# Where a product's weights lie, and in which order high and low parts are multiplied: two edits to a transformer block on one core

## The chip, the core and the metric

The kernel runs on one core of a Trainium2 chip. The metric is device time in microseconds (us) of one execution. The kernel before takes 967.7 us, the median of three runs from 967.39 to 967.99.

A core has a matrix engine (TensorE, PE in the profile; its loading of weights is listed apart as PEld), a vector engine (VectorE, DVE), a scalar engine (ScalarE, ACT), a general engine (GpSimd, POOL) and a queue engine (SyncE, SP) that issues loads. They work side by side and wait for each other through semaphores. Matrix products accumulate in banks of a memory called PSUM; the other tiles lie in SBUF, 128 partitions wide.

## The reference

One layer over 256 tokens of width 2048, all in float32:

```python
h = rmsnorm(x, norm1_g)
q, k, v, u = split(h @ w_in)               # 1536, 512, 512, 512 columns
a = rmsnorm(window_attention(q, k, v, sink))
f = rmsnorm(fourier_mix(u, w_fourier))
x = x + concatenate([a, f]) @ w_out
h = rmsnorm(x, norm2_g)
gate, val = split(h @ w_up)                # 5504 columns each
gate = conv3(gate) + dw_b                  # along the tokens
x = x + (gelu(gate) * val) @ w_down
y = rmsnorm(x, normf_g)
```

Most of the arithmetic is in the four large products: w_in, w_out, w_up and w_down.

## The kernel before

**Float32 products out of parts.** TensorE multiplies a rounded 32-bit format here. So each float32 weight tile is split into a high part (ScalarE copies it into the rounded format, L170 or L910) and a low part (VectorE subtracts the high part from the raw tile, L171 or L911), and so is each activation. A product is the sum of three: high by high, low by high, high by low.

**Where the parts lie.** A weight tile is 128 x 2048. Its two parts share one tile of 2 x 2048 + 128 elements a partition, of which there are three in turn (parts_tile, L138). How many elements the high part is moved in from the tile's start, and the low part from the middle, is a table of four kinds of use:

```python
PLACES = {"still": (0, 16), "first": (16, 16), "moving": (0, 0), "product": (28, 28)}
```

**Two ways to multiply.** In moving_weights (L303) the activation is the stationary operand and 512 columns of weights stream past it, three matmuls for each 128 rows of weights (L309 high by high, L310 low by high, L311 high by low). In still_weights (L315) the weights are stationary and the activation streams: for each of 16 k tiles of 128 rows one matmul of 512 columns with the weights' high part (L320; the 512 are the activation's 256 high and 256 low columns) and one of 256 columns with their low part (L321; the high columns alone). The two halves of the 512 are added when the bank is emptied. All go into one PSUM bank, the first clearing it.

**The stages, in order.** u and v with moving weights; then 16 units of still weights for k and q, one k and three q for each of four groups, with the attention's small products (scores, transposes, values) and the Fourier mix's placed between the units; then w_out with moving weights in 16 steps; then the feed-forward part.

**The feed-forward part** is a written list of items (ff_items, L64). 86 of them are up-projections (gate and val of 43 tiles, still weights, L1105). 56 are products of the down-projection (L1109): w_down for the first 32 tiles is taken in four groups, and each group by a scheme of seven products per column half (names P1, P7, N5, N3, P6, P2, N4) whose operands are sums of blocks. by_parts (L1010) multiplies one: its four blocks take three matmuls of 512 columns each (L1014 to L1016), with the operand stationary. Items 0 and 1 are gate0 and val0, item 2 is gate1, which stands behind four small float32 matmuls that spread the second norm's scales (L293). The list goes on with still units up to val7, and then each group opens with three of them and alternates product and still unit ("uuu" + "su" * 13 + "s"). Behind the four groups come four late down-projections with moving weights, six more still units, four more late down-projections and the last columns.

**What sets the order around it.** Each engine runs its instructions in the order written. Behind each item on TensorE ff_step (L941) empties earlier banks, splits the weights of the item two further on and issues the loads for later ones on SP's queue; some products' sums of raw weights are made by accumulating loads on POOL's queue (L915, L917, L926). At the end of a column half shared_out (L996) adds eight 128 x 512 tiles on VectorE.

The functions that the edit touches:

Of the kernel before, what the change touches and what calls it, by code (L numbers as in the profile page):

```python
# [15 lines left out]
S = 256  # L16
NK = D // P
# [46 lines left out]
def ff_items():  # L64


    def ups(tiles):
        return [(kind, j) for j in tiles for kind in ("gate", "val")]

    items = ups(range(8))  # L70
    for g in range(N_GROUPS):
        todo = {
            "u": ups(range(8 * g + 8, 8 * g + 16)),
            "s": [("product", g, c, p) for c in range(2) for p in PRODUCTS[c]],
        }
        items += [todo[c].pop(0) for c in PATTERN]
        assert not any(todo.values())
    items += [("down", 0, c) for c in range(4)] + ups(LAST)
    items += [("down", 1, c) for c in range(4)] + [("last", c) for c in range(4)]
    return items  # L80
# [3 lines left out]
def block_kernel(  # L84
# [18 lines left out]
    nc = tc.nc  # L103
# [10 lines left out]
    def bank(pool, name):  # L114
        return pool.tile([P, 512], F32, tag=pool.name, name=name)
# [5 lines left out]
    items, up_index = ff_items(), {}  # L121
# [11 lines left out]
    raws, halves = {}, {}  # L133


    PLACES = {"still": (0, 16), "first": (16, 16), "moving": (0, 0), "product": (28, 28)}

    def parts_tile(name, place):  # L138
        t = wp.tile([P, 2 * 2048 + 128], F32R, tag="parts", name=name, bufs=3)
        oh, ol = PLACES[place]  # L140
        return t[:, oh : oh + 2048], t[:, 2048 + ol : 4096 + ol]

    def load(i, pieces=1):
        if i < len(units) and i not in raws:
            src, n, _ = units[i]
            raws[i] = wp.tile([P, 2048], F32, tag="raw", name=f"raw{i}", bufs=RAW)
            m = n // pieces
            for p in range(pieces):
                s = slice(p * m, (p + 1) * m)
                nc.sync.dma_start(raws[i][:, s], src[:, s])  # L150
                yield
# [50 lines left out]
    first = load(0, 4)  # L202
# [50 lines left out]
    ps = bank(dn, "ps_warm")  # L253
# [49 lines left out]
    def moving_weights(hi, lo, n, kk, act, b, ps, first, last, q0=0):  # L303

        for q, k in enumerate(kk, q0):
            ah = act(k)[:, b * P : (b + 1) * P]
            al = act(k)[:, S + b * P : S + (b + 1) * P]
            wh, wl = hi[:, q * n : (q + 1) * n], lo[:, q * n : (q + 1) * n]
            nc.tensor.matmul(ps, ah, wh, start=first and q == q0, stop=False)  # L309
            nc.tensor.matmul(ps, al, wh, start=False, stop=False)  # L310
            nc.tensor.matmul(  # L311
                ps, ah, wl, start=False, stop=last and q == q0 + len(kk) - 1
            )

    def still_weights(hi, lo, ps, kk):  # L315

        for k in kk:
            h = hT[k // 4][:, k % 4, :]
            s = slice(k * P, (k + 1) * P)
            nc.tensor.matmul(ps, hi[:, s], h, start=k == 0, stop=False)  # L320
            nc.tensor.matmul(  # L321
                ps[:, 0:S], lo[:, s], h[:, 0:S], start=False, stop=k == NK - 1
            )

    def hk(k):
        return hT[k // 4][:, k % 4, :]

    later = []  # L330

# [13 lines left out]
    def at(when, i, f, *a):  # L345
        when.setdefault(i, []).append((f, a))
# [5 lines left out]
    def unit(i, work):  # L352
        run(before, i)
        work(*halves.pop(i))
        run(beside, i)
        step(i)
        run(behind, i)
# [6 lines left out]
    for k in range(NK):  # L364
        c, q = k // 4, k % 4
# [4 lines left out]
        hi, lo = halves[c]  # L370
# [187 lines left out]
    for c in range(4):  # L558

        def work(hi, lo):  # L560
            for b in range(2):
                moving_weights(
                    hi, lo, 512, range(4 * c, 4 * c + 4), hk, b, ps_v[b], c == 0, c == 3
                )

        unit(N_V + c, work)
# [139 lines left out]
    for n, (kind, h) in enumerate(QK_ORDER):  # L706

        def work(hi, lo):
            ps = st["ps", kind, h] = bank(mm, f"ps_{kind}{h}")
            still_weights(hi, lo, ps, range(NK))  # L710

        unit(N_QK + n, work)

# [49 lines left out]
    for n, (c, kq) in enumerate(OUT_ORDER):  # L763
# [15 lines left out]
        if kq >= 2:  # L779
            part = "a" if kq == 2 else "f"  # L780
            ps = ps_a[c] if kq < 3 else ps_a[c, "f"]
# [113 lines left out]
    def ring_load():  # L895
        if ring_next[0] < len(ring):
            key = ring[ring_next[0]]
            ring_next[0] += 1
            ring_tiles[key] = fp.tile([P, 2048], F32, tag="rawd", name="rawd%d%d%s" % key)
            nc.sync.dma_start(ring_tiles[key], weights_of(*key))  # L900
# [20 lines left out]
    def first_sums(g, c):  # L921

        a, b = ring_tiles[g, c, "a"], ring_tiles[g, c, "b"]
        x = ring_tiles["x"] = fp.tile([P, 2048], F32, tag="sumw", name=f"sumw{g}{c}", bufs=1)
        nc.vector.tensor_tensor(x, a, b, ALU.add)
        nc.gpsimd.dma_start(b, weights_of(g, c, "d"), accum_op=ALU.add)  # L926
# [14 lines left out]
    def ff_step(n):  # L941
        todo, later[:] = list(later), []
        for f in todo:
            next(f, None)
        run(beside, n)
        split_item(n + 2)
        for f in todo:
            for _ in f:
                pass
        run(behind, n)  # L950

    def up_posts(n, kind, j, ps):
        if kind == "gate":
            at(beside, n + 1, scaled_sum, ps, f"g{j}")
            at(beside, n + 2, gate_conv, j)
            at(behind, n + 2, gate_gelu, j)
        else:
            at(beside, n + 1, scaled_sum, ps, f"v{j}")
            at(beside, n + 2, val_mult, j)
            if j % 8 == 7 and j < 8 * N_GROUPS:  # L960
                g = j // 8
                at(behind, n + 1, operand, g, "P1")
                at(behind, n + 2, operand, g, "N4")
                at(behind, n + 3, operand_sums, g, 0)
                at(behind, n + 4, operand, g, "P7")
                at(behind, n + 4, operand, g, "P2")
                at(behind, n + 5, operand_sums, g, 1)
                at(behind, n + 5, operand, g, "N5")
                at(behind, n + 6, operand, g, "N3")
                at(behind, n + 7, operand, g, "P6")  # L970
            if j >= 8 * N_GROUPS:
                at(behind, n + 2, act_parts, j)
# [37 lines left out]
    def by_parts(ps, o, hi, lo, first, last):  # L1010

        for p in range(4):
            s = slice(p * 512, (p + 1) * 512)
            nc.tensor.matmul(ps, o[:, 0, p, :], hi[:, s], start=first and p == 0, stop=False)  # L1014
            nc.tensor.matmul(ps, o[:, 1, p, :], hi[:, s], start=False, stop=False)  # L1015
            nc.tensor.matmul(ps, o[:, 0, p, :], lo[:, s], start=False, stop=last and p == 3)  # L1016
# [58 lines left out]
    for q in range(2):  # L1075
        kind, j = items[q]
        ps = bank(mm, f"ps_{kind}{j}")
# [6 lines left out]
    for ps, hi, lo in pair:  # L1084
        still_weights(hi, lo, ps, range(12, NK))
# [7 lines left out]
    for n, it in enumerate(items):  # L1093
        if n < 2:
            continue
        if it[0] == "last":
            break
        if n in (8, 9):
            ring_load()
        if n == 13:  # L1100
            pending.append(lambda: first_sums(0, 0))
        if it[0] in ("gate", "val"):
            kind, j = it
            ps = bank(mm, f"ps_{kind}{j}")
            still_weights(*halves.pop(up_index[n]), ps, range(NK))  # L1105
            ff_step(n)
            up_posts(n, kind, j, ps)
            continue
        if it[0] == "product":  # L1109
            kind, g, c, p = it  # L1110
            end = g == N_GROUPS - 1
            if (c, p) in held:
                by_parts(held[c, p], parts[p], *halves.pop(it), g == 0, end)
            else:
                ps = bank(mm, f"ps_{p}{g}{c}")
                by_parts(ps, parts[p], *halves.pop(it), True, True)
                at(beside, n + 1, product_out, g, c, p, ps)
            if end and p == "N4":
                at(behind, n + 1, shared_out, c)
        else:  # L1120
            kind, g, c = it
            hi, lo = halves.pop(up_index[n])
            ps = [bank(mm, f"ps_l{g}{c}{b}") for b in range(2)]
            for b in range(2):
                moving_weights(hi, lo, 512, LATE[g], act.get, b, ps[b], True, True)
            at(beside, n + 1, down_out, c, ps)
            if (g, c) == (0, 0):
                gfb = fp.tile([P, D], F32, tag="sumw", name="gfb", bufs=1)
                nc.gpsimd.dma_start(gfb, normf_g.partition_broadcast(P))
        ff_step(n)  # L1130
# [149 lines left out]
```

## Time and profile before

| What | Value |
|---|---|
| median of three runs | 967.7 us |
| the profiled execution's own time | 967.03 us |
| its span, first to last instruction | 965.3 us |
| TensorE busy | 955.1 us, 5089 matmuls |
| VectorE busy | 745.0 us |
| ScalarE busy | 540.0 us |
| GpSimd busy | 44.6 us |
| mean granted TensorE clock | 0.998 |
| moved by DMAs | 211.59 MB, mean 219 GB/s |

The page counts an engine as busy while an instruction of it is listed as running. Matmuls overlap, so a busy TensorE may still be issuing more slowly than it could; the distance between the starts of two matmuls is read from the timeline, and a stretch of the table of stretches gives it for many at once. The chain is the work that ended last, followed backwards from releaser to releaser.

### The profile page before, as it was taken

To read this page: it belongs to the slowest core of one execution; us is meant where nothing else is said; L and a number is where in the kernel's file an instruction comes from. 1 tells how busy PE (TensorE), PEld (TensorE's weight loads), DVE (VectorE), ACT (ScalarE), POOL (GpSimd) and SP (SyncE) were. 2 spreads that over 40 slices of the span, in tenths; PEclk is the share of its full clock that TensorE was granted. 3 is DMA by queue.
4 is the path that set the end of the run, shared out by engine and by line. 5 is a ranking of instruction groups with operands and counts; after the bars stand their busy time and mean duration, and the time that the engine had idled before them with its cause. 6 is when DMAs were issued, how large, how long until landed. Compare 5 with 4: busy or idle time off the path is not lost.

```text
span 965.3 us, 12801 instructions
## 1 busy us (share of the span) xinstructions
PE 955.1 (99%) x5089; PEld 820.1 (85%) x5089; DVE 745.0 (77%) x924; ACT 540.0 (56%) x654; POOL 44.6 (5%) x59
## 2 busy tenths in 40 slices
PE   9999999999999999999999999999999999999996
PEld 7789998888888888888888888888888888888885
DVE  5668877666576689787898877988778979878674
ACT  6756766554455446556565555665555655553534
POOL 0000000000000000000000000000000000000003
PEclk9999999999999999999999999999999999999999
DMA  8854444446456676977778787876977686775532
GB/s 320 338 189 155 175 138 168 142 167 215 177 177 243 233 220 194 288 226 256 225 253 240 235 293 231 261 236 206 290 245 245 206 278 213 227 225 210 209 132 88
DMA packets 33548, 211.59 MB, mean 219 GB/s; under 512 B 3792, under 2 KB 4304, under 8 KB 9424
## 3 DMA queue, kind: packets, MB, share of 16 engines
q1 hardware_dynamic: 29744, 184.54, 51.8%
q0 software_dynamic: 3600, 26.22, 14.5%
q8 instruction: 40, 0.66, 0.3%
q14 instruction: 20, 0.16, 0.0%
q10 hardware_dynamic: 144, 0.01, 0.0%
HBM read 208.65 MB, written 2.10 MB: 218 GB/s over the span
## 4 chain that ended last, share of the span: by engine, by line
PE 98%; DMA 1%; ACT 0%; SPq 0%; POOL 0%; issue 0%; DVE 0%; ACTq 0%; POOLq 0%
PE ps_val L320 16%; PE ps_gate L320 16%; PE ps_gate L321 8%; PE ps_val L321 8%; PE ps_q L320 5%; PE ps_P L1015 3%; PE ps_P L1014 3%; PE ps_P L1016 3%; PE ps_N L1015 2%; PE ps_q L321 2%; PE ps_N L1014 2%; PE ps_a L311 2%; PE ps_a L309 2%; PE ps_a L310 2%; PE ps_N L1016 2%; PE ps_k L320 2%
## 5 line engine op out<-in xcount | busy, mean ns | idle before, releaser
L171 DVE TENSOR_TENSOR parts<-raw,parts 128x2048 fp32r<-128x2048 f32 (+3 forms) x145 | 313.0, 2159 | 63.7 <-ACT parts L170 63.5
L170 ACT ACTIVATE parts<-raw 128x2048 fp32r<-128x2048 f32 (+3 forms) x144 | 262.0, 1819 | 75.4 <-PE ps_l L311 25.7
L320 PE MATMUL ps_gate<-hU,parts 128*128 128x512 f32 x688 | 242.2, 394 | 0.0
L320 PE MATMUL ps_val<-hU,parts 128*128 128x512 f32 x688 | 242.2, 394 | 0.0
L321 PE MATMUL ps_gate<-hU,parts 128*128 128x256 f32 x688 | 192.7, 280 | 0.0
L321 PE MATMUL ps_val<-hU,parts 128*128 128x256 f32 x688 | 192.7, 280 | 0.0
L320 PEld LDWEIGHTS ps_val<-hU,parts 128*128 128x128 f32 x688 | 129.3, 188 | 29.8
L320 PEld LDWEIGHTS ps_gate<-hU,parts 128*128 128x128 f32 x688 | 129.3, 188 | 29.7
L321 PEld LDWEIGHTS ps_gate<-hU,parts 128*128 128x128 f32 x688 | 129.2, 188 | 1.1
L321 PEld LDWEIGHTS ps_val<-hU,parts 128*128 128x128 f32 x688 | 129.1, 188 | 1.1
L805 ACT ACTIVATE ft_g<-ps_gate 128x256 f32<-128x256 f32 x43 | 16.6, 385 | 124.2 <-PE ps_gate L321 124.2
L805 ACT ACTIVATE ft_v<-ps_val 128x256 f32<-128x256 f32 x43 | 16.6, 386 | 97.5 <-PE ps_val L321 97.5
L320 PE MATMUL ps_q<-hT,parts 128*128 128x512 f32 x192 | 66.9, 393 | 0.0
L321 PE MATMUL ps_q<-hT,parts 128*128 128x256 f32 x192 | 53.2, 277 | 0.0
L1015 PE MATMUL ps_P<-parts_P,op_P 128*128 128x512 f32 x128 | 50.9, 398 | 0.0
L1014 PE MATMUL ps_P<-parts_P,op_P 128*128 128x512 f32 x128 | 50.2, 392 | 0.0
L1016 PE MATMUL ps_P<-parts_P,op_P 128*128 128x512 f32 x128 | 49.6, 387 | 0.0
L911 DVE TENSOR_TENSOR parts_N<-sumw,parts_N 128x2048 fp32r<-128x2048 f32 x16 | 36.6, 2290 | 10.1 <-ACT parts_N L910 10.1
L320 PEld LDWEIGHTS ps_q<-hT,parts 128*128 128x128 f32 x192 | 36.1, 188 | 7.3
L807 DVE TENSOR_TENSOR fa_g<-ps_gate,ft_g 128x256 f32<-128x256 f32 x43 | 18.1, 421 | 29.0 <-ACT ft_g L805 29.0
L1015 PE MATMUL ps_N<-parts_N,op_N 128*128 128x512 f32 x96 | 38.2, 398 | 0.0
L309 PE MATMUL ps_a<-parts,cat 128*128 128x512 f32 x96 | 37.9, 395 | 0.0
(323 smaller groups left out, 1591.9 us busy)
## 6 DMA issues: line engine op xcount, KB each, us to landing
raw<-in_w_up SPq DMA_DIRECT2D x86, 1024.0 KB, 5.0
raw<-in_w_in SPq DMA_DIRECT2D x21, 1024.0 KB, 5.0
raw<-in_w_out SPq DMA_DIRECT2D x16, 1024.0 KB, 4.8
sumw<-in_w_down POOLq DMA_DIRECT2D x16, 1024.0 KB, 8.6
raw<-in_w_down_late SPq DMA_DIRECT2D x8, 1024.0 KB, 4.8
raw<-in_w_down_last SPq DMA_DIRECT2D x4, 768.0 KB, 4.3
raw<-in_w_in SPq DMA_DIRECT2D x8, 256.0 KB, 6.6
xs<-in_x SPq DMA_DIRECT2D x4, 512.0 KB, 10.7
```

Of the source, the lines that this page charges most:

```text
L170: nc.scalar.activation(hi[:, s], raw[:, s], AF.Copy)
L171: nc.vector.tensor_tensor(lo[:, s], raw[:, s], f32(hi[:, s]), ALU.subtract)
L309: nc.tensor.matmul(ps, ah, wh, start=first and q == q0, stop=False)
L310: nc.tensor.matmul(ps, al, wh, start=False, stop=False)
L311: nc.tensor.matmul(ps, ah, wl, start=False, stop=last and q == q0 + len(kk) - 1)
L320: nc.tensor.matmul(ps, hi[:, s], h, start=k == 0, stop=False)
L321: nc.tensor.matmul(ps[:, 0:S], lo[:, s], h[:, 0:S], start=False, stop=k == NK - 1)
L805: nc.scalar.activation(tmp, ps[:, S : 2 * S], AF.Copy)
L911: nc.vector.tensor_tensor(lo, src, f32(hi), ALU.subtract)
L1014: nc.tensor.matmul(ps, o[:, 0, p, :], hi[:, s], start=first and p == 0, stop=False)
L1015: nc.tensor.matmul(ps, o[:, 1, p, :], hi[:, s], start=False, stop=False)
L1016: nc.tensor.matmul(ps, o[:, 0, p, :], lo[:, s], start=False, stop=last and p == 3)
```

## The change

Two things. The table's entry for products becomes (0, 0), so both parts of a product's weights begin where those of a moving tile do. And still_weights gets a parameter lag. With lag 0 the order of its 32 matmuls is what it was: high part of k tile 0, low part of 0, high of 1, low of 1 and so on. With lag 4 it opens with the high parts of tiles 0 to 4, goes on with the low part of 0, the high part of 5, the low part of 1, the high part of 6, and ends with the low parts of 11 to 15. All 16 units of q and k are made with lag 4, and of the feed-forward items number 2 alone. The set of matmuls, their operands' contents, the bank, the loads and the splits stay as they are.

```diff
-    PLACES = {"still": (0, 16), "first": (16, 16), "moving": (0, 0), "product": (28, 28)}
+    PLACES = {"still": (0, 16), "first": (16, 16), "moving": (0, 0), "product": (0, 0)}
...
-    def still_weights(hi, lo, ps, kk):
-
-        for k in kk:
+    def still_weights(hi, lo, ps, kk, lag=0):
+
+
+        todo = [("hi", k) for k in kk[: lag + 1]]
+        for n, k in enumerate(kk):
+            todo.append(("lo", k))
+            todo += [("hi", q) for q in kk[lag + 1 + n : lag + 2 + n]]
+        for part, k in todo:
             h = hT[k // 4][:, k % 4, :]
             s = slice(k * P, (k + 1) * P)
-            nc.tensor.matmul(ps, hi[:, s], h, start=k == 0, stop=False)
-            nc.tensor.matmul(
-                ps[:, 0:S], lo[:, s], h[:, 0:S], start=False, stop=k == NK - 1
-            )
+            if part == "hi":
+                nc.tensor.matmul(ps, hi[:, s], h, start=k == 0, stop=False)
+            else:
+                nc.tensor.matmul(
+                    ps[:, 0:S], lo[:, s], h[:, 0:S], start=False, stop=k == NK - 1
+                )
...
-            still_weights(hi, lo, ps, range(NK))
+            still_weights(hi, lo, ps, range(NK), lag=4)
...
-            still_weights(*halves.pop(up_index[n]), ps, range(NK))
+            still_weights(*halves.pop(up_index[n]), ps, range(NK), lag=4 if n == 2 else 0)
```

## The prediction

> **What bounds the kernel now.** I read the page's busy shares and its chain first, then the table of stretches, then the TensorE rows of the timeline around the edges between units.
>
> ```profile
> span 965.3 us, 12801 instructions
> PE 955.1 (99%) x5089; PEld 820.1 (85%) x5089; DVE 745.0 (77%) x924; ACT 540.0 (56%) x654; POOL 44.6 (5%) x59
> PE 98%; DMA 1%; ACT 0%; SPq 0%; POOL 0%; issue 0%; DVE 0%; ACTq 0%; POOLq 0%
> L320 PE MATMUL ps_gate<-hU,parts 128*128 128x512 f32 x688 | 242.2, 394 | 0.0
> L321 PE MATMUL ps_gate<-hU,parts 128*128 128x256 f32 x688 | 192.7, 280 | 0.0
> ```
>
> TensorE holds 98% of the chain, so the end moves only if TensorE's matmuls follow each other faster or if it is made to wait. The mean durations (394 and 280 ns) are not the price of a matmul, since they overlap; the price is the distance from one start to the next. The table of stretches gives it for whole units. I call a call of still_weights over 16 k tiles a still unit (16 wide matmuls of 512 columns, 16 narrow ones of 256).
>
> ```profile
> core 0: us, PE busy (x) PEld busy (x) DVE busy (x) ACT busy (x) POOL busy (x), PEclk, DMA share, GB/s
> 68.80:74.48 5.68, 5.68 (x35) 4.99 (x34) 3.30 (x8) 3.48 (x6) 0.75 (x1) 1.00 0.54 180
> 81.82:87.42 5.60, 5.60 (x34) 4.91 (x33) 4.63 (x18) 3.36 (x6) 0.75 (x1) 1.00 0.53 187
> 130.63:136.07 5.44, 5.44 (x35) 4.81 (x33) 4.37 (x11) 4.45 (x9) 0.74 (x1) 1.00 0.44 179
> 294.51:328.11 33.60, 33.60 (x194) 29.44 (x193) 22.49 (x28) 15.51 (x18) 0.00 (x0) 1.00 0.68 251
> 375.69:476.17 100.48, 100.48 (x531) 85.81 (x529) 80.06 (x79) 57.83 (x54) 4.35 (x5) 1.00 0.78 242
> 736.00:864.00 128.00, 128.00 (x680) 109.57 (x679) 112.12 (x125) 74.98 (x75) 5.62 (x7) 1.00 0.76 237
> 886.43:919.09 32.66, 32.66 (x193) 28.96 (x192) 22.17 (x26) 15.56 (x18) 0.00 (x0) 1.00 0.55 193
> 919.09:940.88 21.79, 21.79 (x99) 18.02 (x97) 15.40 (x17) 9.18 (x8) 0.00 (x0) 1.00 0.43 145
> ```
>
> Rows four and seven are the same work, six gate and value units each (192 matmuls; the counts include neighbours that reach in), at the same granted clock of 1.00: 33.60 against 32.66 us. Rows one to three are one q, one k and one q unit, 5.68, 5.60 and 5.44 us. So a still unit has two paces: 5.44 us (0.340 a pair) and 5.60 us (0.350 a pair), and the pace isn't set by load on the chip, since both occur side by side in one stage with DVE and the DMAs about as busy. What sets it is seen at the edges of units.
>
> ```profile
> 375.69 0.39 PE L1014 MATMUL ps_P<-parts_P,op_P 128*128 128x512 f32 x1
> 375.92 0.40 PE L1015 MATMUL ps_P<-parts_P,op_P 128*128 128x512 f32 x1
> 376.16 0.39 PE L1016 MATMUL ps_P<-parts_P,op_P 128*128 128x512 f32 x1
> 376.38 0.39 PE L1014 MATMUL ps_P<-parts_P,op_P 128*128 128x512 f32 x1
> ...
> 378.46 0.39 PE L320 MATMUL ps_gate<-hU,parts 128*128 128x512 f32 x1
> ...
> 384.06 0.39 PE L1014 MATMUL ps_N<-parts_N,op_N 128*128 128x512 f32 x1
> ```
>
> A product (12 wide matmuls, weights in place 28) takes 378.46 - 375.69 = 2.77 us, 0.69 for each three, and the still unit behind it keeps the long pace: 384.06 - 378.46 = 5.60. Now the same two shapes where the parts lie in place 0, the late down-projections (L309 to L311) and the still units that follow them:
>
> ```profile
> 886.20 0.39 PE L311 MATMUL ps_l<-parts,act 128*128 128x512 f32 x1
> 886.43 0.39 PE L320 MATMUL ps_gate<-hU,parts 128*128 128x512 f32 x1
> ...
> 886.78 0.39 PE L320 MATMUL ps_gate<-hU,parts 128*128 128x512 f32 x1
> ...
> 891.89 0.39 PE L320 MATMUL ps_val<-hU,parts 128*128 128x512 f32 x1
> 897.33 0.39 PE L320 MATMUL ps_gate<-hU,parts 128*128 128x512 f32 x1
> ...
> 919.09 0.39 PE L309 MATMUL ps_l<-parts,act 128*128 128x512 f32 x1
> 921.84 0.39 PE L309 MATMUL ps_l<-parts,act 128*128 128x512 f32 x1
> 924.56 0.39 PE L309 MATMUL ps_l<-parts,act 128*128 128x512 f32 x1
> ```
>
> The first still unit behind them begins with one long pair (886.43 to 886.78, 0.35), settles to the short pace and takes 5.46; the next takes 5.44 (897.33 - 891.89), and the pace lasts for six units. The first down half after a short-paced still unit takes 2.75, the second 2.72.
>
> **The change part by part, against the profiled execution** (967.03 us: span 965.3 and 1.73 around it; the median of the runs, 967.7, is 0.67 higher). No instruction is added or removed on any engine and no DMA moves in its queue; offsets and the order on TensorE change.
>
> (a) Products in place 0. A product's triple is the triple of the down-projection: operand's high part on high weights, low part on high weights, high part on low weights, all 512 wide, with weights in the same tile at the same offsets, and the late act tiles even share the products' operand buffers. So I take its rows. Before, twelve pairs of product and still unit take 100.48 us, 8.373 a pair. After: 2.75 + 5.46 = 8.21, so 0.167 less (8.373 - 8.206 with three decimals of the starts). A still unit follows 55 of the 56 products: 55 x 0.167 = 9.2 us, and 0.1 for the last product and the down-projection behind it. Six more still units stand second or third in a group's opening three and keep the pace they are handed: 6 x 0.16 = 1.0 us. Bounds: if the pace doesn't change, a product alone gains at most 2.77 - 2.72 = 0.05, with 56 of them 2.8 us, and at worst its matmuls all take the dearest distance shown (375.92 to 376.16, 0.24: 2.88 a product, +6 us).
>
> (b) The first full gate unit (item 2). It stands behind four small fp32 matmuls and starts into the long pace; the last row here is of the table of stretches:
>
> ```profile
> 271.67 0.61 PE L293 MATMUL ps_spread<-diag,ones 128*128 128x128 f32 x4
> 272.03 0.47 PE L320 MATMUL ps_gate<-hU,parts 128*128 128x512 f32 x1
> ...
> 272.46 0.40 PE L320 MATMUL ps_gate<-hU,parts 128*128 128x512 f32 x1
> ...
> 272.81 0.40 PE L320 MATMUL ps_gate<-hU,parts 128*128 128x512 f32 x1
> 272.03:367.31 95.28, 95.28 (x547) 83.51 (x546) 71.03 (x86) 47.45 (x57) 1.05 (x1) 1.00 0.64 221
> ```
>
> The pair from 272.46 to 272.81 is a long one, and the last row, a stretch of 17 still units up to the first product, makes 5.60 each: the sixteen behind item 2 (val1 to gate9) inherit its pace. Five wide matmuls in a row are a short piece of the all-wide run after which the units at 886 went short; no row shows this very opening, so its worth lies between 0 and 16 x 0.16 = 2.6 us. I take 2.6, by the nearest row, the wide run ahead of 886.43. The unit itself: 4 of its distances become wide to wide and 4 at its end narrow to narrow, shown in the last column piece:
>
> ```profile
> 955.99 0.28 PE L1152 MATMUL ps_e<-hi,act 128*128 128x256 f32 x1
> 956.11 0.28 PE L1153 MATMUL ps_e<-lo,act 128*128 128x256 f32 x1
> ```
>
> 0.12 against the 0.113 of the short pace: 4 x 0.007 = 0.03 us dearer.
>
> (c) q and k. Of 16 units nine are, by their starts, of the kind of row three above and seven of the kind of rows one and two (fp32 matmuls ahead add 0.1 to either). If the opening makes all short, the seven gain 7 x (0.16 - 0.02 to settle - 0.03) = 0.8 and the nine lose 9 x 0.03 = 0.3: 0.5 us gained. If it makes all long, the nine lose 9 x 0.16 and the seven nothing: 1.5 us lost. I take the gain of 0.5, for the reason in (b). The order also lets the low half of the weights come 1 us later, but the page's rows show 0.0 idle at L320 and L321, so no stall goes and no wait is late behind it.
>
> (d) What gets closer. DVE is 112.1 of 128.0 us busy in the densest group (row six); 2% less time makes 89%, not a bound. The tightest place is behind the eight sums of shared_out:
>
> ```profile
> 817.32 2.28 DVE L911 TENSOR_TENSOR parts_N<-sumw,parts_N 128x2048 fp32r<-128x2048 f32 x1
> 820.05 0.39 PE L1016 MATMUL ps_N<-parts_N,op_N 128*128 128x512 f32 x1
> 874.60 1.28 DVE L1021 TENSOR_TENSOR xs<-ps_l,xs 128x512 f32<-128x512 f32 x2
> 875.43 0.47 PE L309 MATMUL ps_l<-parts,act 128*128 128x512 f32 x1
> sumw<-in_w_down POOLq DMA_DIRECT2D x16, 1024.0 KB, 8.6
> ```
>
> The low part lands at 819.60, 0.45 us ahead of its use at 820.05; about two pairs are run faster while DVE works off its sums, so some 0.3 of it goes. At 875.43 TensorE already waits for a bank that DVE empties, and that wait grows by 0.1. With a unit thrown into the long pace by such a wait I put 0.3 us on it, between 0 and 1.5 (0.3 in each of the four groups and 0.3 there). POOL's accumulating loads land 8.6 us after issue and have two pairs, 16.4 us, to do so; SP's queue only issues the same loads earlier, at a DMA share of 0.78.
>
> Sum: 9.3 + 1.0 + 2.6 + 0.05 (item 2 itself) + 0.5 - 0.3 = 13.1 us; 967.03 - 13.1 = 953.9, and 0.67 for the median: 954.6 us.
>
> **The rivals.** Rule of no effect: a matmul's distance hangs on its columns alone. Then neither edit moves anything: 967.7. Against it stand 33.60 and 32.66 us for the same columns, and 0.24 beside 0.23 within one product. The Trainium skill, "SBUF — State Buffer", section "Who interferes with whom", says that TensorE has two independent read ports, for moving operand and weights, and never waits on another engine; by it an offset would be worth 0 and the time 967.7. The trace doesn't agree: equal work has two paces here. I give this 0.07.
>
> Products reset the pace but the five-wide opening doesn't: item 2 to gate9 stay long (2.6 lost against the sum) and q and k lose 0.3 in place of gaining 0.5: 954.6 + 2.6 + 0.8 = 958.0. For it: behind small matmuls, fp32 or narrow, the units of rows one and two went long while others went short, so such a start is easily tipped. Chance 0.20.
>
> Products reset only some of their followers, half say, because a product of 12 from the long pace is only just settled: 954.6 + 0.5 x 9.2 + up to 2 = 960 to 962. Against it: at 886.43 parts in place 0 send their follower short at once. Chance 0.14.
>
> The other side: in the new place the still unit behind a product falls into a third, dearer pace, 0.24 a wide and 0.12 a narrow matmul, the dearest shown: 16 x 0.36 = 5.76 against 5.60, 55 times: 8.8 us, 976. It decides from 0.04 us a unit on (1.9 us in all). Nothing shows such a pace for a whole unit; chance 0.09.
>
> **How the numbers follow.** Forecast 0.50 at 954.6; its own range is 952.5 (units and products without the 0.02 to 0.03 of settling, 2.1 us) to 956. Then 0.20 at 958.0, 0.14 at 960 to 962, 0.07 at 967.7, 0.09 at 976. The range 952.5 to 961.5 leaves out some 0.2. About 0.2% (1.9 us) is what a measurement can tell from no change. Faster is 0.50 + 0.20 + 0.14 = 0.84, within 0.2% 0.06, and slower 0.10 (0.09 and a hundredth of the no-effect case with q and k long).
>
> **What would show it.** Right: product to product 8.21 us instead of 8.37 around 375 us, triples of 0.68, still units of 5.44 from item 2 on, the stretch that is now 736 to 864 us down from 128.0 to some 125.4 us (14 pairs and two more still units), every q and k unit at 5.47 to 5.58. Wrong in (a): 5.60 behind a product; in (b): 5.60 from val1 to gate9 and short only behind the first product; in (d): idle time in front of L1014, L1016 or L320. The prediction fails if the pace hangs on the weights' address in a way that products and down-projections don't share.

## The result and the profile after

The changed kernel takes 955.01 us (median of four runs, 954.15 to 955.46) against 967.85 (four runs, 967.39 to 968.18) on the same chip: a ratio of 0.9867, with a 95% interval of 0.9850 to 0.9884. It is 12.8 us faster; forecast were 954.6 us and a gain of 13.1.

The profiled execution is the longest of the four, 955.46 us. First, as in the prediction, the page's span, busy shares and shares of the chain:

```profile
span 953.7 us, 12801 instructions
PE 943.7 (99%) x5089; PEld 813.7 (85%) x5089; DVE 745.2 (78%) x924; ACT 540.4 (57%) x654; POOL 44.6 (5%) x59
PE 95%; DMA 2%; DVE 1%; ACT 1%; issue 0%; SPq 0%; POOL 0%; ACTq 0%; POOLq 0%
```

The same instructions, the same busy time on DVE, ACT and POOL within 0.4 us, and TensorE busy 11.4 us less: it is still the bound, and its matmuls follow each other faster.

Where the time went is in the table of stretches. The first four rows are of the kernel before, the next four the same stretches of the changed one: the q and k units with the small products between them, the sixteen units val1 to gate9, the first group of products, and the third group.

```profile
57.00:165.35 108.35, 108.35 (x686) 97.83 (x686) 84.70 (x191) 70.34 (x135) 8.13 (x11) 1.00 0.45 156
277.71:367.31 89.60, 89.60 (x514) 78.52 (x513) 65.67 (x82) 44.12 (x52) 1.05 (x1) 1.00 0.66 230
367.31:478.94 111.63, 111.63 (x586) 95.22 (x585) 90.32 (x90) 66.86 (x65) 4.35 (x5) 1.00 0.77 240
607.37:735.80 128.43, 128.43 (x682) 109.93 (x681) 107.21 (x110) 72.82 (x70) 5.25 (x6) 1.00 0.79 246
```

```profile
57.98:166.13 108.15, 108.15 (x688) 97.74 (x686) 84.63 (x191) 70.38 (x136) 8.11 (x11) 1.00 0.43 156
278.53:365.57 87.04, 87.04 (x515) 77.15 (x513) 65.47 (x82) 44.20 (x52) 1.05 (x1) 1.00 0.67 237
365.57:475.00 109.43, 109.43 (x587) 94.30 (x585) 90.32 (x89) 66.86 (x65) 4.34 (x5) 1.00 0.77 244
600.77:726.54 125.77, 125.77 (x681) 108.74 (x680) 107.16 (x110) 72.90 (x70) 5.24 (x6) 1.00 0.79 251
```

The sixteen units make 5.44 each (87.04 / 16) where they made 5.60. The first group is 2.20 us shorter, the third 2.66; the second equals the third (128.43 to 125.77), and the fourth went from 128.43 to 126.06. Together the four groups give 9.9 us, the sixteen units 2.56, q and k 0.20, and item 2 0.1 (5.68 to 5.58): 12.8 in all, as much as the medians show. The six units behind the first late down-projections take 32.66 as before. The spans differ by 11.6 only (965.3 to 953.7), because the first stage, up to the first matmul for v, took 29.78 us in this execution and 28.64 in the one before. Its instructions are the same in all kernels of this case, and it took from 27.8 to 29.8 us in them, so this is not put down to the change.

The edges of units on the timeline (start, length, engine and line): item 2's opening, a product with the still unit behind it, and the next product.

```profile
272.95 1.40 PE L326 MATMUL ps_gate<-hU,parts 128*128 128x512 f32 x5
274.19 0.28 PE L328 MATMUL ps_gate<-hU,parts 128*128 128x256 f32 x1
...
365.57 0.39 PE L1019 MATMUL ps_P<-parts_P,op_P 128*128 128x512 f32 x1
...
368.31 0.39 PE L326 MATMUL ps_val<-hU,parts 128*128 128x512 f32 x1
...
368.66 0.39 PE L326 MATMUL ps_val<-hU,parts 128*128 128x512 f32 x1
...
373.77 0.39 PE L1019 MATMUL ps_P<-parts_P,op_P 128*128 128x512 f32 x1
```

A product takes 368.31 - 365.57 = 2.74 us and the unit behind it 5.46, its first pair a long one (0.35): 8.20 for the two, where the forecast had 8.21. Keep that first long pair in mind: item 2 already went short, so the product stands behind a short-paced unit here, and yet the unit behind the product has to settle anew.

The two waits of the forecast's last term, first the product behind shared_out's eight sums with VectorE's split beside it, then the bank at the down-projection (the bracket is idle time and what ended it):

```profile
808.77 0.40 PE L1020 MATMUL ps_N<-parts_N,op_N 128*128 128x512 f32 x1
809.12 0.50 PE L1021 MATMUL ps_N<-parts_N,op_N 128*128 128x512 f32 x1
809.47 0.40 PE L1019 MATMUL ps_N<-parts_N,op_N 128*128 128x512 f32 x1
...
863.25 0.39 PE L311 MATMUL ps_l<-parts,act 128*128 128x512 f32 x1
863.84 0.47 PE L309 MATMUL ps_l<-parts,act 128*128 128x512 f32 x1 [0.20 <-DVE xs L1026]
```

```profile
806.78 2.29 DVE L916 TENSOR_TENSOR parts_N<-sumw,parts_N 128x2048 fp32r<-128x2048 f32 x1
```

The low part ends at 806.78 + 2.29 = 809.07 and TensorE takes it at 809.12. Its distance is 0.35 there where it was 0.23 to 0.24, the next one as well, and the product takes 3.02 us instead of 2.74: 0.28 lost. At the bank the distance is 0.59 where it was 0.51.

### The profile page after: what moved, and what is told of

Same layout as the page of the kernel before. It is cut to its first block, busy times and chain, and to the rows that moved or that the text cites. A ratio compares the mean times of both kernels' runs of the same rounds, so it can differ in the third digit from the quotient of the medians.

```text
span 953.7 us, 12801 instructions
## 1 busy us (share of the span) xinstructions
PE 943.7 (99%) x5089; PEld 813.7 (85%) x5089; DVE 745.2 (78%) x924; ACT 540.4 (57%) x654; POOL 44.6 (5%) x59
## 4 chain that ended last, share of the span: by engine, by line
PE 95%; DMA 2%; DVE 1%; ACT 1%; issue 0%; SPq 0%; POOL 0%; ACTq 0%; POOLq 0%
PE ps_gate L326 16%; PE ps_val L326 16%; PE ps_val L328 8%; PE ps_gate L328 8%; PE ps_q L326 5%; PE ps_P L1020 3%; PE ps_P L1019 3%; PE ps_P L1021 3%; PE ps_q L328 2%; PE ps_a L311 2%; PE ps_a L309 2%; PE ps_a L310 2%; PE ps_N L1019 2%; PE ps_N L1020 2%; PE ps_N L1021 2%; DMA raw<-in_w_in 2%
## 5 line engine op out<-in xcount | busy, mean ns | idle before, releaser
L326 PE MATMUL ps_val<-hU,parts 128*128 128x512 f32 x688 | 236.8, 390 | 0.0
L326 PE MATMUL ps_gate<-hU,parts 128*128 128x512 f32 x688 | 236.4, 390 | 0.0
L328 PE MATMUL ps_val<-hU,parts 128*128 128x256 f32 x688 | 190.4, 277 | 0.0
L328 PE MATMUL ps_gate<-hU,parts 128*128 128x256 f32 x688 | 189.8, 277 | 0.0
L326 PE MATMUL ps_q<-hT,parts 128*128 128x512 f32 x192 | 61.3, 393 | 0.0
L328 PE MATMUL ps_q<-hT,parts 128*128 128x256 f32 x192 | 45.6, 278 | 0.0
L1020 PE MATMUL ps_N<-parts_N,op_N 128*128 128x512 f32 x96 | 37.7, 392 | 0.0
L1019 PE MATMUL ps_N<-parts_N,op_N 128*128 128x512 f32 x96 | 37.6, 392 | 0.0
```

The lines of the kernel that those rows point to most:

```text
L328: nc.tensor.matmul(ps[:, 0:S], lo[:, s], h[:, 0:S], start=False, stop=k == NK - 1)
```

## The experiments

No kernel here leaves out part of the computation. Diffs are against the changed kernel, unless said otherwise. The first four ran on one chip, beside the kernel before at 967.08 us there; the last four on another, beside it at 967.28.

**The place alone.**

```diff
-            still_weights(hi, lo, ps, range(NK), lag=4)
+            still_weights(hi, lo, ps, range(NK), lag=0)
...
-            still_weights(*halves.pop(up_index[n]), ps, range(NK), lag=4 if n == 2 else 0)
+            still_weights(*halves.pop(up_index[n]), ps, range(NK), lag=0)
```

> Products in place 0, every still unit in the old order (high, low, high, low), item 2 and q and k too. My theory, that a run of wide matmuls with weights in place 0 leaves the next still unit in the short pace and that otherwise the pace is handed on: item 2 to gate9 stay at 5.60 us, every unit behind the first product takes 5.46, a product 2.75; the time is that of the changed kernel plus 2.7 for item 2 to gate9 and 0.2 for q and k, about 957.9. Rival, that the pace of the whole feed-forward part is set by the opening of item 2 and the products' place adds nothing: still units stay at 5.60 throughout, about 967.

957.62 us (957.41 to 958.23), a ratio of 0.9905 (0.9889 to 0.9922): 9.5 us faster than before. Stretches for val1 to gate9 and the third group, and the starts of the first product, the unit behind it, and the second product:

```profile
277.96:367.56 89.60, 89.60 (x514) 78.39 (x513) 65.68 (x82) 44.12 (x52) 1.05 (x1) 1.00 0.65 229
602.79:728.57 125.78, 125.78 (x682) 108.75 (x681) 107.14 (x110) 72.90 (x70) 5.25 (x6) 1.00 0.80 251
```

```profile
367.56 0.40 PE L1019 MATMUL ps_P<-parts_P,op_P 128*128 128x512 f32 x1
...
370.33 0.39 PE L326 MATMUL ps_val<-hU,parts 128*128 128x512 f32 x1
...
375.79 0.39 PE L1019 MATMUL ps_P<-parts_P,op_P 128*128 128x512 f32 x1
```

The sixteen units stay long, 89.60. The first product comes out of the long pace and takes 2.77; the unit behind it is short already, 5.46, and the groups are those of the changed kernel. So a product in place 0 resets the pace, whatever it is handed.

**The order alone.**

```diff
-    PLACES = {"still": (0, 16), "first": (16, 16), "moving": (0, 0), "product": (0, 0)}
+    PLACES = {"still": (0, 16), "first": (16, 16), "moving": (0, 0), "product": (28, 28)}
```

> The order of the change (q, k and item 2 open with five wide matmuls), products in place 28 as before. Two theories differ most here. First: a product in place 28 itself throws the unit behind it into the long pace; then item 2 to gate9 are short (5.44), the first product ends that, every unit behind it takes 5.60, and the time is 967.85 - 2.7 - 0.2 = 964.9. Second: such a product only hands on the pace it finds, and was long before because it was handed the long one; then every still unit to the end is short, 5.44 to 5.46, and the time is between 953 and 956, the products' place adding next to nothing.

952.39 us (951.69 to 952.51), a ratio of 0.9848 (0.9833 to 0.9862): 14.7 us faster than before, where the change as a whole gained 12.8. The intervals of the two ratios overlap (0.9850 to 0.9884 there), so the totals alone do not settle which is faster; the stretches do: the four groups together are 2.4 us shorter than in the changed kernel (the sum stands further down). The first group, the third and the fourth, and the same edges on the timeline:

```profile
364.20:473.00 108.80, 108.80 (x586) 94.08 (x585) 90.20 (x89) 66.74 (x65) 4.35 (x5) 1.00 0.78 245
598.12:723.24 125.12, 125.12 (x681) 108.51 (x680) 107.07 (x110) 72.90 (x70) 5.26 (x6) 1.00 0.80 252
723.24:848.82 125.58, 125.47 (x682) 108.51 (x680) 112.66 (x126) 75.25 (x76) 5.83 (x7) 1.00 0.77 243
```

```profile
364.20 0.39 PE L1019 MATMUL ps_P<-parts_P,op_P 128*128 128x512 f32 x1
...
366.92 0.39 PE L326 MATMUL ps_val<-hU,parts 128*128 128x512 f32 x1
...
367.26 0.39 PE L326 MATMUL ps_val<-hU,parts 128*128 128x512 f32 x1
...
372.36 0.39 PE L1019 MATMUL ps_P<-parts_P,op_P 128*128 128x512 f32 x1
```

The products still lie in place 28. Handed a short pace by item 2, a product takes 2.72 us and the unit behind it 5.44, from its first pair on (0.34): 8.16 for the two, 0.05 less than in place 0. There is nothing to settle. The same product made 2.77 and its unit 5.60 in the kernel before, where it was handed the long pace. So place 28 does not make the unit behind it long; it hands on what it finds. One unit's opening, 32 matmuls of 5089, is enough to turn all 56 products and the units behind them. That it is item 2's opening and not the new order of q and k is shown by two runs below: item 2 goes short without the latter, and in the last version with products in place 28 the third group takes the same 125.12 us with nine of the 16 q and k units in the old order.

**The order of item 2 without that of q and k.**

```diff
-            still_weights(hi, lo, ps, range(NK), lag=4)
+            still_weights(hi, lo, ps, range(NK), lag=0)
```

> The changed kernel with q and k back in the old order; products in place 0 and item 2 opening with five stay. Expected: the stretch of q and k goes from 108.15 back to 108.35 us, everything from item 2 on as in the changed kernel (item 2 5.57, val1 to gate9 5.44 each); about 955.2 in all. The rival for this part, that five openers are what makes q and k short, would ask for 0.5 us or more here.

955.62 us in one run, span 953.8. The q and k stretch is back at what it was before, the rest as in the changed kernel:

```profile
57.96:166.31 108.35, 108.35 (x687) 97.84 (x686) 84.57 (x191) 70.36 (x136) 8.11 (x11) 1.00 0.44 156
```

The new order is worth 0.20 us over all q and k units. That is read from the stretch; one total cannot tell it.

**Products in place 64**, that is 256 bytes a partition further on than place 0.

```diff
-    PLACES = {"still": (0, 16), "first": (16, 16), "moving": (0, 0), "product": (0, 0)}
+    PLACES = {"still": (0, 16), "first": (16, 16), "moving": (0, 0), "product": (64, 64)}
```

> The changed kernel with the products' parts moved in by 64 elements (256 bytes) instead of 0. If what counts is where an operand starts within 256 bytes (the offsets of all tiles that were seen settled agree modulo 256 bytes), nothing changes: product 2.75, still unit behind it 5.46, 955.0. If any offset against the tile's start costs something, products take 2.77 and the units behind them 5.60 as with place 28: about 964 to 965.

954.22 us in one run. The third group takes what it does with place 0:

```profile
599.61:725.38 125.77, 125.77 (x681) 108.79 (x680) 107.15 (x110) 72.89 (x70) 5.26 (x6) 1.00 0.80 251
```

So it isn't having an offset that matters, but which one.

**Products in place 12.** 28 and 12 elements are 112 and 48 bytes, which differ by 64. If only the place within 64 bytes counted, the two would behave alike.

```diff
-    PLACES = {"still": (0, 16), "first": (16, 16), "moving": (0, 0), "product": (0, 0)}
+    PLACES = {"still": (0, 16), "first": (16, 16), "moving": (0, 0), "product": (12, 12)}
```

> The changed kernel with products in place 12 (48 bytes) in place of 0. If what counts is where the streamed operand starts within 64 bytes, 12 and 28 are the same place (they differ by 64 bytes): a product takes 2.72 us, the unit behind it 5.44, and the time is that of the order alone, about 952 to 953. If it counts within 256 bytes, 12 is a third place and has no reason to be like 28; then products of 2.75 or more and units of 5.46 or more, 955 or above.

954.75 us in one run. The third group, and the first product with the units behind it and the next product:

```profile
600.17:725.85 125.68, 125.68 (x682) 108.78 (x680) 107.08 (x110) 72.94 (x70) 5.24 (x6) 1.00 0.80 251
```

```profile
365.13 0.39 PE L1019 MATMUL ps_P<-parts_P,op_P 128*128 128x512 f32 x1
...
367.89 0.39 PE L326 MATMUL ps_val<-hU,parts 128*128 128x512 f32 x1
...
373.33 0.39 PE L1019 MATMUL ps_P<-parts_P,op_P 128*128 128x512 f32 x1
```

A product takes 2.76, dearer than in either other place behind a short unit, and the unit behind it 5.44 with nothing to settle. It is neither 28 (2.72 and 5.44) nor 0 (2.74 and 5.46). The 64-byte theory falls.

The same trace holds one product in place 12 behind a long unit. In the fourth group a product loses time to a late low part, as in the changed kernel, and here the unit behind it goes long. The starts of that unit, of the product behind it, of the next unit and of the next product:

```profile
810.77 0.40 PE L326 MATMUL ps_val<-hU,parts 128*128 128x512 f32 x1
...
816.38 0.39 PE L1019 MATMUL ps_P<-parts_P,op_P 128*128 128x512 f32 x1
...
819.13 0.39 PE L326 MATMUL ps_gate<-hU,parts 128*128 128x512 f32 x1
...
824.58 0.39 PE L1019 MATMUL ps_N<-parts_N,op_N 128*128 128x512 f32 x1
```

The long unit takes 5.61 by these rounded starts, the product 2.75, and the unit behind it 5.45: the product did not pass the long pace on. In this one instance place 12 behaves as place 0 does, and not as place 28.

**Two wide openers instead of five**, with products in place 28.

```diff
-    PLACES = {"still": (0, 16), "first": (16, 16), "moving": (0, 0), "product": (0, 0)}
+    PLACES = {"still": (0, 16), "first": (16, 16), "moving": (0, 0), "product": (28, 28)}
...
-            still_weights(*halves.pop(up_index[n]), ps, range(NK), lag=4 if n == 2 else 0)
+            still_weights(*halves.pop(up_index[n]), ps, range(NK), lag=1 if n == 2 else 0)
```

> Products in place 28, q and k as in the changed kernel, item 2 opening with two wide matmuls and not five. If the start behind fp32 matmuls needs several wide distances to settle, item 2 stays long and, since products in place 28 hand on the pace that they find, everything to the last product stays at 5.60 and 2.77: about 966.8. If any wide-to-wide distance tips it, it is the time of the order alone, about 952.4.

952.29 us in one run. The start of item 2 on the timeline:

```profile
272.18 0.72 PE L326 MATMUL ps_gate<-hU,parts 128*128 128x512 f32 x2
...
272.86 0.39 PE L326 MATMUL ps_gate<-hU,parts 128*128 128x512 f32 x1
...
273.20 0.39 PE L326 MATMUL ps_gate<-hU,parts 128*128 128x512 f32 x1
```

The first pair behind the opening is short already (272.86 to 273.20, 0.34), and val1 to gate9 take 87.05. One wide matmul out of its turn is enough at item 2; it doesn't take several wide distances there.

**A version built on these**: products in place 28, eleven openers for the two long units k0 and q1, the old order for the q units that had lost by the new one, and shared_out's eight sums split over two units (the edit of its body is not printed).

```diff
-    PLACES = {"still": (0, 16), "first": (16, 16), "moving": (0, 0), "product": (0, 0)}
+    PLACES = {"still": (0, 16), "first": (16, 16), "moving": (0, 0), "product": (28, 28)}
...
+    LAGS = {("k", 0): 10, ("q", 1): 10}
+    LAGS.update({x: 4 for x in (("k", 1), ("k", 2), ("k", 3), ("q", 7), ("q", 10))})
...
-            still_weights(hi, lo, ps, range(NK), lag=4)
+            still_weights(hi, lo, ps, range(NK), lag=LAGS.get((kind, h), 0))
...
-                at(behind, n + 1, shared_out, c)
+                at(behind, n + 1, shared_out, c, 0)
+                at(behind, n + 2, shared_out, c, 1)
```

> Products in place 28 and item 2 opening with five wide matmuls, as in the kernel with the order alone (0.9848 of the kernel before). Added: of q and k only seven units change their order, k1, k2, k3, q7 and q10 with five openers, k0 and q1, which stayed long with five, with eleven; and the eight sums of shared_out are put behind two items, four each. If a wide run of about ten distances is what settles a start behind fp32 matmuls, k0 and q1 come down from 5.69 to 5.60 us or less and the stretch of q and k from 108.15 to about 107.6. If the waits of 0.37 and 0.35 us that the order-only kernel shows at a product's low part and at a down-projection's bank come from the eight sums in one piece, both shrink to 0.1 or less. Together 0.9 to 1.2 us less than the order alone: a ratio of 0.9837. If neither holds, 0.9848.

952.19 us (951.80 to 952.82), a ratio of 0.9845 (0.9829 to 0.9862). It can't be told from the order alone (0.9848). Its q and k stretch, the first late down stage, and the place where the wait went:

```profile
56.96:165.51 108.55, 108.55 (x688) 97.96 (x686) 84.61 (x191) 70.35 (x136) 8.13 (x11) 1.00 0.44 156
849.55:871.34 21.79, 21.79 (x98) 18.02 (x96) 21.32 (x23) 8.10 (x5) 0.00 (x0) 1.00 0.62 226
```

```profile
808.33 0.39 PE L326 MATMUL ps_val<-hU,parts 128*128 128x512 f32 x1
808.86 0.39 PE L328 MATMUL ps_val<-hU,parts 128*128 128x256 f32 x1
```

Choosing orders unit by unit failed. With eleven openers one of the two long units went short and the other did not: k0 is as long with them (5.68) as with five (5.69), while the pairs of q1 behind its openers come at 0.34 (the two starts below). Whether the openers did that is not shown, since the unit ahead of q1 has another order here as well.

```profile
71.78 0.39 PE L326 MATMUL ps_q<-hT,parts 128*128 128x512 f32 x1
...
72.12 0.39 PE L326 MATMUL ps_q<-hT,parts 128*128 128x512 f32 x1
```

As a whole q1 gains only 0.06 (5.63 for 5.69), since the eleven narrow matmuls at its end follow each other at 0.12. And q units that had been short in the old order in the kernel before went long in the old order here, because the units ahead of them had changed; the stretch is 0.4 us longer than in the changed kernel. What a q or k unit does hangs on what came before it. The split sums took away the wait at the late down stage (21.79 for 22.24 in the changed kernel), but the one in the fourth group only moved to the next unit, whose first distance is 0.53.

**The still units' own high parts moved**, by 16 elements, in the kernel before (diff against that one).

```diff
-    PLACES = {"still": (0, 16), "first": (16, 16), "moving": (0, 0), "product": (28, 28)}
+    PLACES = {"still": (16, 16), "first": (16, 16), "moving": (0, 0), "product": (28, 28)}
```

> The kernel before with one edit: the high part of a still unit's weights moved in by 16 elements (64 bytes), like the low part, everything else as before, so products in place 28 and the old order. If the long pace comes of high and low weights that start 64 bytes apart, it goes: every still unit 5.44 to 5.46, 953 to 955. If 64 bytes don't matter, nothing changes and the time is that of the kernel before.

965.50 us in one run, 1.8 below the kernel before. The q and k stretch, val1 to gate9 and the last six units:

```profile
57.28:167.28 110.00, 110.00 (x688) 98.49 (x687) 84.83 (x191) 70.59 (x136) 8.13 (x11) 1.00 0.43 153
280.04:368.79 88.75, 88.75 (x514) 78.25 (x513) 65.65 (x82) 44.11 (x52) 1.05 (x1) 1.00 0.67 231
884.26:917.54 33.28, 33.28 (x194) 29.10 (x192) 22.26 (x27) 15.53 (x18) 0.00 (x0) 1.00 0.53 190
```

Here a third pace appears: 88.75 / 16 = 5.547 us a unit on average from val1 to gate9, and the same 33.28 / 6 = 5.547 behind the late down-projections, where every other kernel of this case has 5.44. The product between such units takes 2.77. The long-paced units of the kernel before gain by it; the q and k units (110.00 for 108.35) and the last six (33.28 for 32.66) lose. So the address of a still unit's weights counts as well, and 64 bytes are not neutral for them.

## Why the prediction was right, and where its reasons were not

**The bound and its mechanism held.** TensorE's starts set the time, still units have two paces at the same granted clock of 1.00, and both edits move units from the long to the short one. The rule of no effect is out: an address alone is worth 9.5 us and an order alone 14.7. By the rule of the Trainium skill that the prediction names there ("SBUF — State Buffer", "Who interferes with whom": two independent read ports for TensorE's operands), read as the prediction reads it, neither would be worth anything; the runs contradict that reading. Whether the two ports ever get in each other's way is not shown by them.

**Term (a), right in size, with a reading that stopped short.** 9.3 + 1.0 us were put on the groups. They lost 9.9, that is 10.2 and the 0.28 of the wait, and in the kernel with the place alone the median fell by 9.5. That products in place 0 reset the pace was right. What was read too narrowly is the edge in place 28: "the still unit behind it keeps the long pace" is a true description of the kernel before, but the sum made the products' place the only way out of that pace in the groups and let item 2's opening count for the sixteen units ahead of the first product alone. Place 28 is only the carrier: with a short pace ahead of it the same product and its unit take 8.16 us. The trace of before held no product behind a short unit, so it could not tell a place that makes the pace long from one that passes it on, and no rival asked. The forecast's number could not suffer from this, because the change has both edits.

**Hence the parts don't add up.** The place alone gains 9.5, the order alone 14.7, both 12.8. In the sum, (b) was worth 2.6 because (a) had already paid for the groups. Taken the other way round, item 2's opening alone pays for everything up to the late down-projections, and place 0 then costs: 0.05 for a product and the unit behind it, 8.21 against 8.16. Over four groups that is 109.43 - 108.80, twice 125.77 - 125.12 and 126.06 - 125.58 in the fourth: 2.4 us. The range's lower end had named this case ("without the 0.02 to 0.03 of settling, 2.1 us"), but as a kinder outcome of the change and not as what leaving the products where they were would give.

**Term (b), right**: 2.56 for 2.6, at the upper end of its bounds, and 0.1 gained on item 2 itself where 0.05 was put. Its reason ("a short piece of the all-wide run") is not borne out: two wide openers do the same at item 2, and eleven don't at k0. The value was chosen between bounds of 0 and 2.6, and that it came out at the top is in part luck.

**Term (c), right in sign and mis-sized**: 0.20 for 0.5. The same three units as in the prediction's first table of stretches (one q, one k, one q; 5.68, 5.60 and 5.44 before):

```profile
69.97:75.66 5.69, 5.69 (x36) 4.98 (x35) 3.32 (x8) 3.47 (x6) 0.74 (x1) 1.00 0.52 186
83.02:88.53 5.51, 5.51 (x35) 4.85 (x33) 4.54 (x18) 3.32 (x5) 0.75 (x1) 1.00 0.56 190
131.65:137.15 5.50, 5.50 (x35) 4.84 (x34) 4.43 (x11) 4.45 (x9) 0.74 (x1) 1.00 0.48 186
```

By their starts five of the seven long units went short and gained 0.55 us together; two, that of the first row and the first k unit (5.69 as well), stayed long behind the very opening that turned item 2. The nine others lost 0.33, as put (0.3).

**Term (d), right in size, in part by luck.** The runs lost 0.28 at the product behind shared_out and 0.08 at the bank, for 0.3 put on all of it and 0.1 of that on the bank. But the working let some 0.3 of the 0.45 us of lead go, which leaves 0.15 and no wait at that product, and put the rest on a unit thrown into the long pace. In the changed kernel the lead was used up: the low part was due at 809.00 (808.77 and a distance of 0.23) and ended at 809.07, and the unit behind that product took 5.47, no more than its neighbours' 5.46. A unit did go long behind such a wait with products in place 12. No other wait appeared; the groups take the same time whether or not the units ahead of them are fast, so loads and splits kept up.

**Two prices of rivals** don't come out of their own working, though neither came true. 954.6 + 0.5 x 9.2 + up to 2 is 959.2 to 961.2, not 960 to 962. And 976 is the 967.7 of the kernel before with 8.8 added, without the 3.1 us that (b) and (c) would still have gained.

## What to carry to other kernels

Where a kernel is bound by matmuls, compare the start-to-start distance of equal units in different places of the trace before looking for stalls: here TensorE was busy for 99% of the span, and 1.5% of the time lay in a pace that units hand to each other. When a pace is handed on, look for the first unit that sets it, and change that one before changing the many that pass it on; test such edits one at a time, since two that turn the same units don't add up and one can cost part of what the other gains.

## What the runs showed of the hardware that was not expected

All at a granted clock of 1.00, with the same matmuls.

- A still unit of 16 wide and 16 narrow matmuls keeps one of two paces until something resets it: 5.44 or 5.60 us. With its high parts 64 bytes further on it has a third, 5.547 on average, both behind item 2 and behind the late down-projections.
- A product of 12 wide matmuls between such units passes the pace on from place 28 (2.77 in the long one, 2.72 in the short one), and from place 0 forces the short one behind either, at 0.05 us for product and unit; place 64, tried behind the short pace, costs the same. From place 12 it takes 2.76 with 5.44 for the unit behind it when handed the short pace, and by rounded starts 2.75 and 5.45 in the one instance where it was handed the long one.
- One wide matmul out of its turn turned item 2 short (val1 to gate9 87.05 for 89.60). Behind similar small matmuls, with ten out of their turn, the pairs of q1 were short (0.34) and k0 stayed long (5.68).

Why an address or an order does this stays open: the traces show when matmuls start, not what they wait for. Not tried were other places with the two parts moved apart, a product in place 64 behind a long unit, and another turn of the three tiles that hold the parts.
